# A two-layer hybrid decoder on one core: weighted sums as one 512-column and one 256-column product per head, and four weight granules a layer split by casting and adding DMA

## The chip, the cores and the metric

The kernel runs on one core of one Trainium2 chip. The metric is the time of one execution in device microseconds (us); of several runs the median is given. The profile comes from one execution that the hardware profiler recorded. In it PE is TensorE (matrix products), PEld its loading of weights, DVE is VectorE, ACT is ScalarE, POOL is GpSimd, and SP issues most DMAs.

## The reference, cut to what matters

Two layers, each with a token mixer (two kinds of attention, eight heads each of 64 columns) and a SwiGLU block, both with a residual and a layer norm. There are 256 tokens and 1024 columns, in float32.

```
for l in range(DEPTH):                       # 2
    mix = hybrid_mixer(x, w_in[l], w_branch_sb[l], w_branch_moba[l], w_out[l])
    x = layer_norm(DEEPNORM_ALPHA * x + mix, ...)
    ffn = swiglu(x, w_gate[l], w_up[l], w_down[l])
    x = layer_norm(DEEPNORM_ALPHA * x + ffn, ...)

hybrid_mixer: proj = x @ w_in  ->  q,k,v (stick-breaking) | q,k,v (MoBA) | two gates
    o_sb = weights_sb @ v_sb      # weights_sb: stick-breaking, strictly causal
    o_mb = weights_mb @ v_mb      # weights_mb: softmax, causal (one block of 256)
    merged = sigmoid(g_sb) * (o_sb @ w_branch_sb) + sigmoid(g_mb) * (o_mb @ w_branch_moba)
    return merged @ w_out
```

The change concerns the two weighted sums, `weights @ v`, and the way in which some pieces of the weight matrices get ready.

## The kernel before, in words

**Split operands.** Every float32 operand of a matrix product is split in two parts of the type fp32r: `hi` is the value cast, `lo` is the value minus `hi`. A product is then hi·hi + hi·lo + lo·hi, three matmuls that add into one PSUM bank (`mm3`, line 334).

**Weights.** All weights are laid out by the host as granules of 128 x 1024 floats (512 KB), 122 to a layer, in the order of their use. `WeightStream` (line 100) takes a granule through three steps: SP loads it into one of six `raw` buffers (line 137), ACT casts it into the ring `whi` (line 163), DVE subtracts to give the ring `wlo` (line 167). The rings hold ten granules; a place comes free when the granule that held it has been used (`after`, line 124). Where the weights are the stationary operand (`feat_major`, line 390) a granule takes 24 matmuls of 256 columns; where the tokens are (`tok_major`, line 366) 12 of 512.

**Order.** The program is written out by `Weave` (line 38). The main line issues the projections; attention, rotary embedding, splits and norms are generators that `yield` the time at which they want to go on. The planner advances its own clock with each matmul and keeps planned end times for ACT and DVE, from simple costs (n/1200 + 0.08 us on ACT, n/960 + 0.06 us on DVE). It decides only the order in which instructions are written; on the chip each engine runs its own in that order, and waits on semaphores.

**Attention.** A line treats two pairs of heads (`sb_line` line 505, `mb_line` line 535; two lines of each kind a layer). For each pair: `scores`, then weights on ACT and DVE (in `sb_line` with a small POOL memset of `keep`, line 521, ahead of DVE's scans), then `weighted` (line 460): PE transposes the weights into a bank pair (`_pT`), ACT and DVE split them into `_phi` and `_plo`, and `product_line` (line 479) multiplies. Its stationary operand is v of a head with hi and lo parts side by side, 64 + 64 columns, so that rows 0 to 63 of the result belong to v's hi and rows 64 to 127 to v's lo. A query of the first half sees 128 keys, one of the second half 256. So each head takes four matmuls: the first half of v with 256 columns of `hi`, and with 256 of `lo`; the second half with 128 of each. Both heads of a pair go to one bank `o` of the pool `psC`, which has two banks; the transposes of the rotary embedding, of norms and of SwiGLU take turns in the same two. ACT copies the lower rows (`low`), DVE adds the upper ones (`both`), and the sum is split in its turn.

A tile of 128 x 2 x 384 floats (`wide_work`, tag A, four buffers) holds `keep`, `beta`, `e`, `phi` or `plo` in turn.

Of the kernel before, what the change touches and what calls it, by code (L numbers as in the profile page):

```python
# [7 lines left out]
F32 = mybir.dt.float32  # L8
F32R = mybir.dt.float32r
# [21 lines left out]
NG_LAYER = 122  # L31
EARLY = [*range(8), 8, 14, 9, 15, 20, 24, 21, 25, *range(10, 14), *range(16, 20), 22, 23, *range(26, 40)]
NACT = 12
NWIDE = 4
NTOK_FC = 4


# [62 lines left out]
class WeightStream:  # L100
# [3 lines left out]
    def __init__(self, nc, pool, w, total, weave, rings):  # L104
        self.nc, self.pool, self.w, self.total, self.weave = nc, pool, w, total, weave
        self.loaded, self.split = 0, NWHOLE
        self.done = -1
        self.current = 0
        self.rings = rings
        self._lay()  # L110
        self.dma_t = 1.7
        self.raw, self.parts, self.there, self.ready = {}, {}, {}, {}

    def _lay(self):

# [16 lines left out]
    def load(self, upto, between=lambda g, i: None):  # L132
        while self.loaded < min(upto, self.total):
            g = self.loaded
            t = self.pool.tile([P, GCOLS], F32, tag="raw", name=f"raw{g}", bufs=NRAW)
            for i, sl in enumerate(self._pieces(g)):
                self.nc.sync.dma_start(t[:, sl], self.w[place(g), :, sl])
                between(g, i)
            self.raw[g] = t
            self.dma_t = max(self.dma_t, self.ready.get(g - NRAW, 0.0) + 0.5) + 1.46  # L140
            self.there[g] = self.dma_t + 1.0
            self.loaded += 1

    def line(self):

        nc, weave = self.nc, self.weave
        while self.split < self.total:
            g = self.split
            ahead = g - self.current
            if self.after[g] > self.done:  # L150
                yield weave.t + 0.1
                continue
            if ahead >= LEAD and max(weave.dve_t, weave.act_t) > weave.t + BACKLOG:
                yield weave.t + 0.2
                continue
# [12 lines left out]
            self.parts[g], self.ready[g] = (hi, lo), e
            self.split += 1
            self.load(g + 1 + NRAW)  # L170
# [5 lines left out]
    def take(self, g):  # L176
        self.current = max(self.current, g)
        while self.split <= g:
            self.weave._step(self.side)
        self.weave.t = max(self.weave.t, self.ready[g])  # L180
        return self.parts[g]

# [2 lines left out]
RING = 10 * GCOLS + LINES  # L185
NRAW = 6
NWHOLE = 2
X_AFTER = {(0, 1): ((1, 0), (0, 1)), (1, 1): ((1, 1), (0, 2)), (2, 1): ((1, 2),)}
NSPLIT = 10
HOLD = 8  # L190
# [23 lines left out]
def hybrid_trunk_kernel(ctx: ExitStack, tc: tile.TileContext, w, xT_in, x_in, ln_in,  # L214
# [21 lines left out]
        return work.tile(shape, F32, tag="T", name=name, bufs=3)  # L236

    def wide_work(name, dt=F32):
        return work.tile([P, 2, 384], dt, tag="A", name=name, bufs=NWIDE)

    def bankM(name, shape):
        return psM.tile(shape, F32, tag="M", name=name)

    def bankC(name, shape):
        return psC.tile(shape, F32, tag="C", name=name)

    taken = [False]

    def banksB(name):
        return psB.tile([P, 2, 512], F32, tag="B", name=name)  # L250
# [164 lines left out]
    def rope_line(name, ps, t, put):  # L415

        tmp = small_work(f"{name}_tok{t}", [P, 8, DH])
        e = act(pe_done(), WIDTH, nc.scalar.copy, tmp, ps.rearrange("p (h d) -> p h d", d=DH))
        yield e
        half = ROPE // 2  # L420
        a = small.tile([P, 8, ROPE], F32, tag="ra", name=f"{name}_ra{t}", bufs=1)
        b = small.tile([P, 8, ROPE], F32, tag="rb", name=f"{name}_rb{t}", bufs=1)
        cc = rope[:, t, 0, None, :].to_broadcast([P, 8, ROPE])
        s0 = rope[:, t, 1, None, :half].to_broadcast([P, 8, half])
        s1 = rope[:, t, 1, None, half:].to_broadcast([P, 8, half])
        mul = nc.vector.tensor_mul
        dve(e, P, mul, a, tmp[:, :, :ROPE], cc)
        dve(e, P // 2, mul, b[:, :, :half], tmp[:, :, half:ROPE], s0)
        dve(e, P // 2, mul, b[:, :, half:], tmp[:, :, :half], s1)
        e = dve(e, 2 * P, nc.vector.tensor_add, tmp[:, :, :ROPE], a, b)  # L430
        yield e + MARGIN
        tp = bankC(f"{name}_tp{t}", [P, NPAIR, P])
        flat = tmp.rearrange("p h d -> p (h d)")
        pe_after(e)
        for p in range(NPAIR):
            transpose(tp[:, p, :], flat[:, p * P:(p + 1) * P])
        yield pe_done()
        yield from put(tp, slice(t * P, (t + 1) * P), pe_done())

    PARTS = ((0, P), (P, 384))  # L440

# [18 lines left out]
    def weighted(name, d, wts, v, oT, es, due=None):  # L460

        yield max(es) + MARGIN
        pTs = [banksB(f"{name}_pT{j}") for j in range(2)]
        pe_after(max(es))
        for pT, wt in zip(pTs, wts):
            for h in range(2):
                for c in range(3):
                    cs = slice(c * P, (c + 1) * P)
                    transpose(pT[:, h, cs], wt[:, h, cs])
        e = pe_done()  # L470
        yield e
        for j in range(2):
            parts = [wide_work(f"{name}_p{n}{j}", F32R) for n in ("hi", "lo")]
            e = yield from split_line(*parts, pTs[j][:, :, :384], 768, e)
            if j == 1:
                taken[0] = False
            weave.start(product_line(f"{name}_o{j}", 2 * d + j, parts, v, oT, e, due))

    def product_line(name, p, parts, v, oT, e, due):

        yield e + MARGIN
        while due is not None and len(due) < 2:
            yield weave.t + 0.1
        pe_after(e)
        o = bankC(name, [P, 2, S])
        for h in range(2):
            va, vb = (x[:, 2 * p + h].rearrange("p a c -> p (a c)") for x in v)
            for n, part in enumerate(parts):
                mm(o[:, h, :], va, part[:, h, :S], h == n == 0, False)
            for n, part in enumerate(parts):  # L490
                mm(o[:, h, P:], vb, part[:, h, S:], False, h == n == 1)
        e = pe_done()
        yield e
        if not oT:
            oT.extend(pair_tiles(name[:4] + "o", [P, NPAIR, S]))
        low = small_work(f"{name}_low", [P, 2, S])
        both = small_work(f"{name}_both", [P, S])
        e = act(e, 2 * S, nc.scalar.copy, low[:DH], o[DH:])
        yield e
        for h, r in enumerate(ROWS):  # L500
            e = dve(e, S, nc.vector.tensor_add, both[r], o[:DH, h, :], low[:DH, h, :])
        yield e
        yield from split_line(oT[0][:, p, :], oT[1][:, p, :], both, S, e)

    def sb_line(name, d, q, q_there, ps, v, oT, done):
# [9 lines left out]
        ws_, fs = [], []  # L515
        for s, e in zip(ss, es):
            yield e
            keep, beta = (wide_work(f"{name}_{n}{len(ws_)}") for n in ("keep", "beta"))
            e1 = act(e, 768, nc.scalar.activation, keep, s[:, :, :384], AF.Sigmoid, scale=-1.0)
            e2 = act(e, 768, nc.scalar.activation, beta, s[:, :, :384], AF.Sigmoid)  # L520
            e1 = weave.pool(e1, nc.gpsimd.memset, keep[:, :, P - 1::2 * P], 0.0)
            ws_.append((keep, beta))
            fs.append((e1, e2))
# [11 lines left out]
    def mb_line(name, d, q, k, v, oT, before, done, scored):  # L535
# [16 lines left out]
        for (s, nmax), e in zip(work_, fs):  # L552
            yield e
            ssum = small.tile([P, 2, 2], F32, tag="ssum", name=f"{name}_ssum{len(es)}")
            ex = wide_work(f"{name}_e{len(es)}")
            for h in range(2):
                for n, (a, b) in enumerate(PARTS):
                    e = act(e, b - a + 300, nc.scalar.activation, ex[:, h, a:b], s[:, h, a:b], AF.Exp,
                            bias=nmax[:, h, n:n + 1], accum_out=ssum[:, h, n:n + 1])
            exs.append((ex, ssum))  # L560
            es.append(e)
# [377 lines left out]
```

## Time and profile before

| what | value |
|---|---|
| median of 3 runs (lowest to highest) | 734.23 us (734.13 to 734.25) |
| the profiled execution's own time | 734.21 us |
| its span, first to last instruction | 732.4 us, mean granted PE clock 0.998 |
| busy DVE, ACT, POOL | 515.6, 384.5, 14.8 us |
| DMA issues on POOL | none |
| layer 0: sb lines from the first scores to their last product | about 43 to 81 us |
| layer 0: mb lines | about 90 to 129 us |
| layer 1: the same two | about 402 to 440, 449 to 489 us |

The span is 1.8 us shorter than the time, which also has what lies before the first and after the last instruction. [...] A row of the timeline has its start, its duration, engine, line, operation and operands; `xN` merges N neighbours.

### The profile page before, as it was taken

The page shows a single profiled execution, that of the slowest core. Times are in us where ns is not written, and L with a number is a line of the kernel's source. Part 1 is how long each engine was busy: PE and PEld are TensorE (multiplying, and loading weights), DVE is VectorE, ACT ScalarE, POOL GpSimd, SP SyncE. Part 2 cuts the span into 40 slices and gives each one's busy share as a digit, 9 for nine tenths or more (in the row PEclk, how much of TensorE's full clock was granted, in tenths as well). Part 3 has the DMA queues.
Part 4 walks back from the last instruction along what each step waited for, and adds up shares of the span by engine and source line. Part 5 has one row for each costly group of instructions (what it writes and reads, how often), then busy time and mean ns, then how long its engine had stood idle before and what let it go on. Part 6 is the DMA issues. An engine that isn't in the chain of part 4 may idle for free.

```text
span 732.4 us, 12739 instructions
## 1 busy us (share of the span) xinstructions
PE 723.1 (99%) x5136; PEld 664.7 (91%) x5136; DVE 515.6 (70%) x723; ACT 384.5 (52%) x570; POOL 14.8 (2%) x30
## 2 busy tenths in 40 slices
PE   9999999999999999999999999999999999999996
PEld 5898999998799999988889989999888999998885
DVE  4988877795886666644578897777578766656416
ACT  5755668743565455533356566675246645445300
POOL 0000000000000000000000000000010000000001
PEclk9999999999999999999999999999999999999999
DMA  8953553863586655476158425457436866554601
GB/s 319 353 202 116 163 191 122 263 241 117 176 279 211 198 201 186 160 273 215 57 177 286 144 96 190 147 158 257 161 115 223 264 203 193 186 172 129 244 1 57
DMA packets 39226, 136.32 MB, mean 186 GB/s; under 512 B 4480, under 2 KB 5504, under 8 KB 39168
## 3 DMA queue, kind: packets, MB, share of 16 engines
q1 hardware_dynamic: 39168, 135.51, 54.9%
q8 instruction: 40, 0.66, 0.3%
q14 instruction: 18, 0.15, 0.1%
HBM read 134.45 MB, written 1.05 MB: 185 GB/s over the span
## 4 chain that ended last, share of the span: by engine, by line
PE 95%; DVE 2%; issue 1%; ACT 1%; POOL 1%; POOLq 0%; DVEq 0%
PE l1pf L328 13%; PE l0pf L328 13%; PE l0pd L328 8%; PE l1pg L328 6%; PE l0pg L328 6%; PE l1pe L328 4%; PE l1pd L328 4%; PE l0pq L328 3%; PE l0pk L328 3%; PE l1pk L328 3%; PE l1pvq L328 3%; PE l1pb L328 3%; PE l0pb L328 3%; PE l1pw L328 2%; PE l0pw L328 2%; PE l0pft L328 2%
## 5 line engine op out<-in xcount | busy, mean ns | idle before, releaser
L56 DVE TENSOR_TENSOR wlo<-raw,whi 128x1024 fp32r<-128x1024 f32 (+1 forms) x244 | 292.1, 1214 | 77.1 <-ACT whi L51 74.2
L51 ACT CAST whi<-raw 128x1024 fp32r<-128x1024 f32 (+1 forms) x244 | 249.8, 1042 | 68.4 <-PE l0pd L328 19.1
L328 PE MATMUL l0pf<-xT_hi,whi 128*128 128x256 f32 x288 | 79.6, 276 | 0.0
L328 PE MATMUL l1pf<-xT_hi,whi 128*128 128x256 f32 x288 | 79.6, 276 | 0.0
L328 PE MATMUL l0pf<-xT_lo,whi 128*128 128x256 f32 x288 | 79.5, 276 | 0.0
L328 PE MATMUL l0pf<-xT_hi,wlo 128*128 128x256 f32 x288 | 79.5, 276 | 0.0
L328 PE MATMUL l1pf<-xT_lo,whi 128*128 128x256 f32 x288 | 79.5, 276 | 0.0
L328 PE MATMUL l1pf<-xT_hi,wlo 128*128 128x256 f32 x288 | 79.5, 276 | 0.0
L328 PEld LDWEIGHTS l0pf<-xT_lo,whi 128*128 128x128 f32 x288 | 54.1, 188 | 0.0
L328 PEld LDWEIGHTS l1pf<-xT_lo,whi 128*128 128x128 f32 x288 | 54.1, 188 | 0.0
L328 PEld LDWEIGHTS l1pf<-xT_hi,whi 128*128 128x128 f32 x288 | 54.1, 188 | 0.0
L328 PEld LDWEIGHTS l0pf<-xT_hi,whi 128*128 128x128 f32 x288 | 54.1, 188 | 0.0
L328 PEld LDWEIGHTS l0pf<-xT_hi,wlo 128*128 128x128 f32 x288 | 54.1, 188 | 0.0
L328 PEld LDWEIGHTS l1pf<-xT_hi,wlo 128*128 128x128 f32 x288 | 54.1, 188 | 0.0
L328 PE MATMUL l1pg<-xT_hi,whi 128*128 128x256 f32 x128 | 36.0, 281 | 0.0
L328 PE MATMUL l0pg<-xT_hi,whi 128*128 128x256 f32 x128 | 36.0, 281 | 0.0
L328 PE MATMUL l1pg<-xT_lo,whi 128*128 128x256 f32 x128 | 35.5, 277 | 0.0
L328 PE MATMUL l1pg<-xT_hi,wlo 128*128 128x256 f32 x128 | 35.5, 277 | 0.0
L328 PE MATMUL l0pg<-xT_lo,whi 128*128 128x256 f32 x128 | 35.5, 277 | 0.0
L328 PE MATMUL l0pg<-xT_hi,wlo 128*128 128x256 f32 x128 | 35.4, 277 | 0.0
L328 PE MATMUL l0pd<-whi,l0h_hi 128*128 128x512 f32 x88 | 34.4, 391 | 0.0
L328 PE MATMUL l0pd<-whi,l0h_lo 128*128 128x512 f32 x88 | 34.3, 389 | 0.0
(403 smaller groups left out, 1763.9 us busy)
## 6 DMA issues: line engine op xcount, KB each, us to landing
raw<-in_w_dram SPq DMA_DIRECT2D x240, 512.0 KB, 4.2
ln<-in_ln_dram SPq DMA_DIRECT2D x8, 512.0 KB, 6.2
raw<-in_w_dram SPq DMA_DIRECT2D x8, 256.0 KB, 4.9
x<-in_x_dram SPq DMA_DIRECT2D x2, 512.0 KB, 5.3
out_dram<-x SPq DMA_DIRECT2D x3, 256.0 KB, 2.0
xT_raw<-in_xT_dram SPq DMA_DIRECT2D x4, 128.0 KB, 4.4
xT_raw<-in_xT_dram SPq DMA_DIRECT2D x2, 256.0 KB, 4.8
out_dram<-x SPq DMA_DIRECT2D x2, 128.0 KB, 1.9
```

Of the source, the lines that this page charges most:

```text
L51: f(*args, **kw)
L56: f(*args, **kw)
L328: nc.tensor.matmul(o, a, b, start=start, stop=stop)
```

## The change

It has two parts, and what goes with them.

1. `weighted` makes one tile for hi and lo of a pair, in blocks of 128 columns that alternate (hi, lo, hi, lo, hi, lo). `product_line` then needs two matmuls a head: the first half of v with four blocks (512 columns), the second half with two (256 columns), which add onto the last 256. Each head has a bank to itself, so a product takes both banks of `psC`. The parts come out side by side: DVE adds v_hi·lo to the copied v_lo·hi, and then v_hi·hi; v_lo·lo is dropped. ACT copies 64 x 256 twice in place of 64 x 512 once; DVE makes four additions in place of two.
2. Granules 18, 27, 35 and 43 of each layer are no longer loaded by SP and split by ACT and DVE. POOL issues a casting DMA into `whi`, writes `wlo` = -`whi` with a `tensor_scalar` of 128 x 1024, and issues a DMA that adds the weights onto `wlo`.
3. The planner gets `turnC`, `holdC`, `freeC`: a product is written only once both banks are free in its plan. Tiles of tag A have twice the size and two buffers in place of four; `keep` and `beta` share one.

```
+BY_DMA = (18, 27, 35, 43)
...
+    def by_dma(self, g):
+        return g % NG_LAYER in BY_DMA
+    def dma_line(self, g):
+        nc, weave = self.nc, self.weave
+        hi, lo = self.parts[g]
+        nc.gpsimd.dma_start(hi, self.w[place(g)], max_dma_last_dim=4096)
+        yield weave.t + 4.5
+        e = weave.pool(weave.t, nc.gpsimd.tensor_scalar, lo, hi.bitcast(F32), -1.0, None, op0=OP.mult)
+        yield e + 1.0
+        nc.gpsimd.dma_start(lo, self.w[place(g)], accum_op=OP.add, max_dma_last_dim=4096)
+        self.ready[g] = weave.t + 5.0
...
     def line(self):
         while self.split < self.total:
+            for g in range(max(self.split, NWHOLE), min(self.split + 6, self.total)):
+                if self.by_dma(g) and g not in self.dma and self.after[g] <= self.done:
...
+                    self.dma[g] = weave.add(self.dma_line(g), weave.t)
...
+    def turnC(n=1):
+        while max(held[-2:][:n]) > weave.t:
+            yield weave.t + 0.1
...
-            parts = [wide_work(f"{name}_p{n}{j}", F32R) for n in ("hi", "lo")]
-            e = yield from split_line(*parts, pTs[j][:, :, :384], 768, e)
+            parts = work.tile([P, 2, 6, P], F32R, tag="A", name=f"{name}_p{j}", bufs=NWIDE)
+            e = yield from split_line(parts[:, :, ::2], parts[:, :, 1::2],
+                                      pTs[j][:, :, :384].rearrange("p h (a c) -> p h a c", c=P), 768, e)
...
+        yield from turnC(2)
         pe_after(e)
-        o = bankC(name, [P, 2, S])
-        for h in range(2):
+        os = [bankC(f"{name}{h}", [P, 2, 2, P]) for h in range(2)]
+        own = holdC(2)
+        for h, o in enumerate(os):
+            o = o.rearrange("p a n c -> p (a n c)")
             va, vb = ...
-            for n, part in enumerate(parts):
-                mm(o[:, h, :], va, part[:, h, :S], h == n == 0, False)
-            for n, part in enumerate(parts):
-                mm(o[:, h, P:], vb, part[:, h, S:], False, h == n == 1)
+            mm(o, va, parts[:, h, :4].rearrange("p a c -> p (a c)"), True, False)
+            mm(o[:, S:], vb, parts[:, h, 4:].rearrange("p a c -> p (a c)"), False, True)
...
-        e = act(e, 2 * S, nc.scalar.copy, low[:DH], o[DH:])
+        for h, o in enumerate(os):
+            e = act(e, S, nc.scalar.copy, low[:DH, h], o[DH:, :, 0, :])
         yield e
-        for h, r in enumerate(ROWS):
-            e = dve(e, S, nc.vector.tensor_add, both[r], o[:DH, h, :], low[:DH, h, :])
+        for h, o in enumerate(os):
+            dve(e, S, nc.vector.tensor_add, low[:DH, h], o[:DH, :, 1, :], low[:DH, h])
+        for h, o in enumerate(os):
+            e = dve(e, S, nc.vector.tensor_add, both[ROWS[h]], o[:DH, :, 0, :], low[:DH, h])
+        freeC(own, e)
```

PE at the first product of layer 0 (`l0sb_o`), before; `l0pk` is the projection that runs around it:

```order
L328 MATMUL l0pk_616<-whi,xT_lo 128x512
L328 MATMUL l0sb_o_661<-l0sb_phi_643,l0vsb_166 128x256
L328 MATMUL l0sb_o_661<-l0sb_plo_644,l0vsb_166 128x256
L328 MATMUL l0sb_o_661<-l0sb_phi_643,l0vsb_167 128x128
L328 MATMUL l0sb_o_661<-l0sb_plo_644,l0vsb_167 128x128
L328 MATMUL l0sb_o_661<-l0sb_phi_643,l0vsb_166 128x256
L328 MATMUL l0sb_o_661<-l0sb_plo_644,l0vsb_166 128x256
L328 MATMUL l0sb_o_661<-l0sb_phi_643,l0vsb_167 128x128
L328 MATMUL l0sb_o_661<-l0sb_plo_644,l0vsb_167 128x128
L328 MATMUL l0pk_616<-whi,xT_hi 128x512
```

The same place on PE after the change:

```order
L372 MATMUL l0pk_633<-whi,xT_lo 128x512
L372 MATMUL l0sb_o_662<-l0sb_p_638,l0vsb_166 128x512
L372 MATMUL l0sb_o_662<-l0sb_p_638,l0vsb_167 128x256
L372 MATMUL l0sb_o_663<-l0sb_p_638,l0vsb_166 128x512
L372 MATMUL l0sb_o_663<-l0sb_p_638,l0vsb_167 128x256
L372 MATMUL l0pk_633<-whi,xT_hi 128x512
```

Eight matmuls in one bank have become four in two. The second product of that line followed this one on PE after 3 `l0pk`, 24 score matmuls and 3 `l0pk`; now 6 `l0pk` stand in the last place.

POOL from its first memsets to those of the sb lines of layer 0, before:

```order
L277 MEMSET ends 128x384
L278 MEMSET ends 128x2
L61 MEMSET l0sb_keep_533 128x2x2
L61 MEMSET l0sb_keep_541 128x2x2
L61 MEMSET l0sb_keep_729 128x2x2
L61 MEMSET l0sb_keep_741 128x2x2
L61 ISA
```

And after (the row `ISA` is a setup instruction of POOL that stands ahead of its first arithmetic, which before was that of a norm):

```order
L321 MEMSET ends 128x384
L322 MEMSET ends 128x2
L156 DMA whi<-in_w_dram 128x1024
L61 ISA
L61 TENSOR_SCALAR wlo<-whi 128x1024
L160 DMA wlo<-in_w_dram 128x1024
L61 MEMSET l0sb_kb_529 128x2x2
L61 MEMSET l0sb_kb_536 128x2x2
L61 MEMSET l0sb_kb_738 128x2x2
```

The three steps of granule 18, and the `ISA`, now stand ahead of the memsets of `keep` (now in the tile `l0sb_kb`). In layer 1 granule 18's three steps stand ahead of that layer's memsets in the same way; the steps of granules 27, 35 and 43 follow the memsets.

DVE behind the first product of layer 0, before:

```order
L56 TENSOR_TENSOR l0sb_o_both<-l0sb_o_661,l0sb_o_low 64x256 x2
L56 TENSOR_TENSOR wlo<-raw_425,whi 128x1024
L56 TENSOR_TENSOR l0sb_s_675<-l0sb_s_675,mask 128x4x128
L56 TENSOR_TENSOR l0sb_s_676<-l0sb_s_676,mask 128x4x128
L56 TENSOR_TENSOR l0sbo_lo<-l0sb_o_both,l0sbo_hi 128x256
```

And after:

```order
L56 TENSOR_TENSOR l0sb_o_low<-l0sb_o_662,l0sb_o_low 64x256
L56 TENSOR_TENSOR l0sb_o_low<-l0sb_o_663,l0sb_o_low 64x256
L56 TENSOR_TENSOR l0sb_o_both<-l0sb_o_662,l0sb_o_low 64x256
L56 TENSOR_TENSOR l0sb_o_both<-l0sb_o_663,l0sb_o_low 64x256
L56 TENSOR_TENSOR wlo<-raw_439,whi 128x1024
L56 TENSOR_TENSOR l0sb_s_673<-l0sb_s_673,mask 128x4x128
L56 TENSOR_TENSOR l0sb_s_674<-l0sb_s_674,mask 128x4x128
L56 TENSOR_TENSOR l0sbo_lo<-l0sb_o_both,l0sbo_hi 128x256
```

Two additions have come in ahead of the split of a granule and of the masks of the next scores.

More of the change, by code (lines that the diff above doesn't have):

```diff
@@ L33 @@
 NACT = 12
-NWIDE = 4
+NWIDE = 2
 NTOK_FC = 4
@@ L111, in __init__ @@
         self.dma_t = 1.7
-        self.raw, self.parts, self.there, self.ready = {}, {}, {}, {}
+        self.raw, self.parts, self.there, self.ready, self.dma = {}, {}, {}, {}, {}
     def _lay(self):
@@ L134, in load @@
             g = self.loaded
+            if self.by_dma(g):
+                self.loaded += 1
+                upto += 1
+                continue
             t = self.pool.tile([P, GCOLS], F32, tag="raw", name=f"raw{g}", bufs=NRAW)
@@ L147, in line @@
         while self.split < self.total:
+            for g in range(max(self.split, NWHOLE), min(self.split + 6, self.total)):
+                if self.by_dma(g) and g not in self.dma and self.after[g] <= self.done:
+                    self.parts[g] = tuple(ring[:, self.place[g]:self.place[g] + GCOLS] for ring in self.rings)
+                    self.dma[g] = weave.add(self.dma_line(g), weave.t)
             g = self.split
+            if g in self.dma:
+                self.split += 1
+                continue
             ahead = g - self.current
@@ L179, in take @@
             self.weave._step(self.side)
+        while g in self.dma and g not in self.ready:
+            self.weave._step(self.dma[g])
         self.weave.t = max(self.weave.t, self.ready[g])
@@ L238, in wide_work @@
     def wide_work(name, dt=F32):
-        return work.tile([P, 2, 384], dt, tag="A", name=name, bufs=NWIDE)
+        return work.tile([P, 2, 2, 384], dt, tag="A", name=name, bufs=NWIDE)
     def bankM(name, shape):
@@ L244, in bankC, with holdC, freeC @@
     def bankC(name, shape):
+        held.append(weave.t)
         return psC.tile(shape, F32, tag="C", name=name)
-    taken = [False]
+    taken, held = [False], [0.0, 0.0]
+    def turnC(n=1):
+        while max(held[-2:][:n]) > weave.t:
+            yield weave.t + 0.1
+    def holdC(n=1):
+        held[-n:] = [1e9] * n
+        return range(len(held) - n, len(held))
+    def freeC(own, e):
+        for i in own:
+            held[i] = e
     def banksB(name):
@@ L431, in rope_line @@
         yield e + MARGIN
+        yield from turnC()
         tp = bankC(f"{name}_tp{t}", [P, NPAIR, P])
+        own = holdC()
         flat = tmp.rearrange("p h d -> p (h d)")
@@ L437, in rope_line @@
         yield pe_done()
-        yield from put(tp, slice(t * P, (t + 1) * P), pe_done())
+        e = yield from put(tp, slice(t * P, (t + 1) * P), pe_done())
+        freeC(own, e)
     PARTS = ((0, P), (P, 384))
@@ L495, in product_line @@
             oT.extend(pair_tiles(name[:4] + "o", [P, NPAIR, S]))
-        low = small_work(f"{name}_low", [P, 2, S])
-        both = small_work(f"{name}_both", [P, S])
-        e = act(e, 2 * S, nc.scalar.copy, low[:DH], o[DH:])
+        low = small_work(f"{name}_low", [P, 2, 2, P])
+        both = small_work(f"{name}_both", [P, 2, P])
+        for h, o in enumerate(os):
+            e = act(e, S, nc.scalar.copy, low[:DH, h], o[DH:, :, 0, :])
         yield e
-        for h, r in enumerate(ROWS):
-            e = dve(e, S, nc.vector.tensor_add, both[r], o[:DH, h, :], low[:DH, h, :])
+        for h, o in enumerate(os):
+            dve(e, S, nc.vector.tensor_add, low[:DH, h], o[:DH, :, 1, :], low[:DH, h])
+        for h, o in enumerate(os):
+            e = dve(e, S, nc.vector.tensor_add, both[ROWS[h]], o[:DH, :, 0, :], low[:DH, h])
+        freeC(own, e)
         yield e
+        both = both.rearrange("p a c -> p (a c)")
         yield from split_line(oT[0][:, p, :], oT[1][:, p, :], both, S, e)
@@ L517, in sb_line @@
             yield e
-            keep, beta = (wide_work(f"{name}_{n}{len(ws_)}") for n in ("keep", "beta"))
+            two = wide_work(f"{name}_kb{len(ws_)}")
+            keep, beta = two[:, 0], two[:, 1]
             e1 = act(e, 768, nc.scalar.activation, keep, s[:, :, :384], AF.Sigmoid, scale=-1.0)
@@ L554, in mb_line @@
             ssum = small.tile([P, 2, 2], F32, tag="ssum", name=f"{name}_ssum{len(es)}")
-            ex = wide_work(f"{name}_e{len(es)}")
+            ex = wide_work(f"{name}_e{len(es)}")[:, 0]
             for h in range(2):
```

## The prediction

> **What bounds the kernel now.** I read the page first: busy times, granted clock, the chain.
>
> ```profile
> PE 723.1 (99%) x5136; PEld 664.7 (91%) x5136; DVE 515.6 (70%) x723; ACT 384.5 (52%) x570; POOL 14.8 (2%) x30
> PEclk9999999999999999999999999999999999999999
> PE 95%; DVE 2%; issue 1%; ACT 1%; POOL 1%; POOLq 0%; DVEq 0%
> ```
>
> PE is busy for 99% of the span at full clock, and 95% of the chain that ended last is PE. A busy PE is not yet a PE at its peak, so the next view is that of PE's waits; these two rows are all of it behind the start.
>
> ```profile
> PE l0a_tp L341 <- DVE xT_lo L56: 0.3, 1, 0.3
> PE l1a_tp L341 <- DVE xT_lo L56: 0.3, 1, 0.3
> ```
>
> PE waits 0.6 us for others in 732.4 us. So a microsecond of PE work that goes is a microsecond of time, as long as nothing else becomes late; and no gain is to be had from DVE or ACT alone.
>
> **The products on PE.** The timeline of PE at the first product of layer 0:
>
> ```profile
> 57.41 0.39 PE L328 MATMUL l0pk<-wlo,xT_hi 128*128 128x512 f32 x1
> 57.64 0.39 PE L328 MATMUL l0pk<-whi,xT_lo 128*128 128x512 f32 x1
> 57.87 0.28 PE L328 MATMUL l0sb_o<-l0sb_phi,l0vsb 128*128 128x256 f32 x1
> ...
> 58.74 0.45 PE L328 MATMUL l0pk<-whi,xT_hi 128*128 128x512 f32 x1
> 59.02 0.40 PE L328 MATMUL l0pk<-wlo,xT_hi 128*128 128x512 f32 x1
> 59.26 0.39 PE L328 MATMUL l0pk<-whi,xT_lo 128*128 128x512 f32 x1
> ```
>
> and at the last product of layer 1:
>
> ```profile
> 487.35 0.28 PE L328 MATMUL l1pg<-xT_lo,whi 128*128 128x256 f32 x1
> 487.46 0.28 PE L328 MATMUL l1pg<-xT_hi,wlo 128*128 128x256 f32 x1
> 487.57 0.28 PE L328 MATMUL l1mb_o<-l1mb_phi,l1vmb 128*128 128x256 f32 x1
> ...
> 488.45 0.34 PE L328 MATMUL l1pg<-xT_hi,whi 128*128 128x256 f32 x1
> 488.62 0.28 PE L328 MATMUL l1pg<-xT_lo,whi 128*128 128x256 f32 x1
> ```
>
> From start to start a 512-column matmul takes 0.23 us and a 256-column one 0.113 us. A product takes 58.74 - 57.87 = 0.87 and 488.45 - 487.57 = 0.88 us, for 1536 columns in all, which at the pitch of the long matmuls would be 0.68. The matmul behind it is late as well: 0.28 us to its successor in place of 0.23, and 0.17 in place of 0.113, so some 0.06 more. The excess fits a weight load per matmul that a 128-column matmul is too short to cover. The new product is 2 x 0.227 + 2 x 0.113 = 0.68 us for the same columns, with every load behind at least 256 columns. There are 16 (two lines of two kinds, two pairs each, two layers; in this tile 32 matmuls make four of them):
>
> ```profile
> L328 PE MATMUL l0sb_o<-l0sb_phi,l0vsb x16: 220/252/332, 57.9 to 80.4; 128*128 128x256 f32 x8, 128*128 128x128 f32 x8
> L328 PE MATMUL l0sb_o<-l0sb_plo,l0vsb x16: 272/280/283, 58.0 to 80.5; 128*128 128x256 f32 x8, 128*128 128x128 f32 x8
> L56 DVE TENSOR_TENSOR l0sb_o_both<-l0sb_o,l0sb_o_low x8: 413/417/418, 59.6 to 81.9; 64x256 f32<-64x256 f32 x8
> L51 ACT COPY l0sb_o_low<-l0sb_o x4: 583/584/584, 58.9 to 80.8; 64x512 f32<-64x512 f32 x4
> ```
>
> Saved: at most 16 x (0.87 + 0.06 - 0.68) = **4.0 us**; if the tail of 0.06 stays and a 512-column matmul costs 0.24, as from 59.02 to 59.26, 16 x (0.87 - 0.70) = 2.7 us. I take 4.0, since pitches of 0.227 and 0.113 hold wherever these shapes follow each other.
>
> **DVE and ACT.** DVE gets two more additions a product, 32 x 0.417 = 13.3 us; ACT two copies for one. A copy of 64 x 256 is not in the trace; the nearest are 0.584 above and this activation of 256 columns:
>
> ```profile
> L51 ACT ACTIVATE l0sf<-l0pf 128x256 f32<-128x256 f32 x18 | 6.9, 385 | 32.2 <-PE l0pf L328 32.2
> L56 DVE TENSOR_TENSOR wlo<-raw,whi 128x1024 fp32r<-128x1024 f32 x240 | 289.4, 1223 | 76.7 <-ACT whi L51 73.8
> L51 ACT CAST whi<-raw 128x1024 fp32r<-128x1024 f32 x240 | 247.4, 1049 | 68.1 <-PE l0pd L328 19.1 <-PE l1pe L328 16.9 <-PE l0pf L328 13.2
> ```
>
> So ACT gets 16 x (2 x 0.385 - 0.584) = 3 us. The eight granules that go to DMA take 8 x 1.223 = 9.8 us off DVE and 8 x 1.049 = 8.4 off ACT. Net DVE +3.5, ACT -5.4: both far under the PE time, so I cost them at nothing, except where PE waits for one product's banks. The tightest place is the second product of a line. After the first ends (57.87 + 0.68 = 58.55), its banks come free after a hop of 0.2, two copies (0.77), four additions (1.67) and two hops: about 61.4. On PE six `l0pk` now stand between scores and second product where three stood:
>
> ```profile
> 61.95 0.27 PE L328 MATMUL l0sb_o<-l0sb_phi,l0vsb 128*128 128x256 f32 x1
> ```
>
> That start moves to 61.95 - 0.25 + 3 x 0.227 = 62.4, so 1 us is left. For the first line this covers the added 0.83 us of additions; without that cover it costs what is missing, once a second product. The smaller number of tag A buffers costs nothing: a line's split parts are written only behind its transposes, which have freed both tiles.
>
> **POOL.** New there: 16 DMA issues, eight `tensor_scalar` of 128 x 1024, and the setup instruction moved forward. Rows that come near:
>
> ```profile
> 0.72 0.42 POOL L277 MEMSET ends<- 128x384 f32 x1 [0.29 <-POOLq L925]
> 1.19 0.10 POOL L278 MEMSET ends<- 128x2 f32 x1
> 46.10 0.11 POOL L61 MEMSET l0sb_keep<- 128x4 f32 x1 [44.80 <-ACT l0sb_keep L51]
> 173.50 1.41 DVE L56 SCALAR_TENSOR_TENSOR x<-x,l0a_nmu,ln 128x512 f32<-128x512 f32 x2 [1.31 <-ACT l0pw L51]
> 173.56 0.75 POOL L61 TENSOR_SCALAR l0a_ve<-l0a_ve 128x1 f32<-128x1 f32 x1 [108.07 <-ACT l0pw L51]
> 405.00 0.11 POOL L61 MEMSET l1sb_keep<- 128x4 f32 x1 [34.37 <-ACT l1sb_keep L51]
> 57.04 0.42 SPq L322 DMA_DIRECT2D x<-in_x_dram  x1
> raw<-in_w_dram SPq DMA_DIRECT2D x240, 512.0 KB, 4.2
> ln<-in_ln_dram SPq DMA_DIRECT2D x8, 512.0 KB, 6.2
> ```
>
> A `tensor_scalar`: 0.32 us for 382 more columns is 0.84 ns a column, so 0.75 + 0.86 = 1.6 us; bounds 0.75 (128 x 1) and 2.5 (columns at twice the price, being read and written). An issue: 0.42 on SP; I take 1 us on POOL, bounds 0.4 and 2. Landing of 512 KB: 4.2 to 6.2 from SP; with a cast I take 5, bounds 4.2 and twice 6.2. The setup is bounded by nothing (the row lies behind 108 us of idle POOL); I take it as hidden behind the landing that follows it.
>
> The place where this can matter is granule 18, whose steps stand ahead of the `keep` memsets. Its ring place comes free when granule 9 has been used, at the first row of each pair here; the second is the last `beta`, the third where PE's transposes of it stand (in layer 0 now at 53.11, since three matmuls ahead of them went behind):
>
> ```profile
> 35.01 0.28 PE L328 MATMUL l0pk<-xT_hi,whi 128*128 128x256 f32 x1
> 50.93 0.96 DVE L56 TENSOR_TENSOR l0sb_beta<-l0sb_beta,l0sb_keep 128x767 f32<-128x767 f32 x1
> 53.11 0.40 PE L328 MATMUL l0pk<-whi,xT_hi 128*128 128x512 f32 x1
> 394.48 0.28 PE L328 MATMUL l1pk<-xT_hi,whi 128*128 128x256 f32 x1
> 409.83 0.96 DVE L56 TENSOR_TENSOR l1sb_beta<-l1sb_beta,l1sb_keep 128x767 f32<-128x767 f32 x1
> 412.58 1.47 PE L341 MATMUL l1sb_pT<-ident,l1sb_beta 128*128 128x128 f32 x12
> ```
>
> The steps on POOL: 35.2 + 1 + 5 + 1.6 + 1 = 43.8, ahead of the memset at 46.10; the memset itself may be 53.11 - 51.89 - 0.2 = 1.0 us late before PE waits. That is a budget of 11.9 us for an estimate of 8.6. Layer 1: from 394.7 to 405.00, plus 412.58 - 410.79 - 0.2 = 1.6, again 11.9. The second DMA lands near 49; PE first uses granule 18 behind 12 transposes (1.3 us) and 12 matmuls, near 57. The other three start some 25 us ahead of use, behind the memsets. Cost: nothing, or one for one beyond the budget.
>
> [...]
>
> **The sum.** 734.2 (the profiled execution; span 732.4 and 1.8 around it; the median is 734.23) - 4.0 + 0.3 for short bank waits = **730.5 us**.
>
> **Rivals.**
>
> *The banks eat the gain.* The planner believes in 0.33 us for an addition (256/960 + 0.06) and 0.29 for a copy where rows show 0.417 and 0.385. For four and two of them it is 0.54 us short; its matmul of 256 columns is 0.109 where 0.113 is measured, which gives back some 0.16 us over the 4 us between two products. Eight second products x 0.38 = 3.0 us; without the allowance of 0.3 that gives 730.2 + 3.0 = 733.2. Against it: the same planner has the same errors now, and PE waits 0.6 us.
>
> *POOL's queue (slower).* If the casting DMA lands in 12.4 us, the steps take 16 us, 4.1 beyond the budget: `keep` is cleared late, DVE's scans stand still with every split queued behind them, and PE waits at the transposes in both layers: 730.5 + 8.2 = 738.7. It decides from steps of 13.8 us on, where 2 x 1.9 eats the gain. For it: no DMA of POOL is in the trace. Against it: two landings of 512 KB are, at 4.2 and 6.2.
>
> *POOL and DVE in each other's way (slower).* The `tensor_scalar` of one column took 0.75 us and ended at 174.31, just as the first of the two DVE operations beside it (173.50 to about 174.25) did. If they exclude each other, DVE loses up to 1.6 us at each of eight, 13 us; uncovered, 743. Cover: DVE idles 76.7 us ahead of splits. [...]
>
> *The matmuls don't get cheaper.* A product stays at 0.93 us, and only additions come in: 734.5. Against it stand all rows of 512 columns.
>
> **How the numbers follow.** Forecast, 729.6 to 732.0: 0.68. Banks, 732.0 to 734.2: 0.12, half of it faster and half same. POOL's queue, 733 to 741: 0.10, of it 0.03 same. Exclusion, or a granule that lands late: 0.05, of it 0.01 same. Matmuls as dear: 0.05, of it 0.03 same. A measurement of this kernel can tell 0.2%, 1.5 us. Faster 0.68 + 0.06 = 0.74; same 0.06 + 0.03 + 0.01 + 0.03 = 0.13; slower 0.13. The range takes in the first two cases, 0.80: 729.6 (the largest saving, no wait, and 0.6 for tails that I may have misjudged) to 734.2.
>
> **What would show it.** Right: 64 matmuls fewer, a product of 0.68 us from start to start, no more than 1 us of PE waits, DVE busy about 519 us, ACT about 379, POOL's memset still near 46 and 405. Wrong: PE waiting at `_o` for DVE (banks), at `sb_pT` for DVE with POOL behind it (queue), at `l0pk` or `l0pg` for a DMA (late granule), or `wlo` rows of DVE well above 1.22 us (exclusion). A `tensor_scalar` over 4.9 us, or a landing over 8.3, would use up the budget by itself.

## The result and the profile after

The changed kernel takes 730.43 us (median of 6 runs, 730.03 to 730.97), the kernel before beside it 734.29 us (6 runs, 734.13 to 735.05): a ratio of 0.9945, 95% interval 0.9933 to 0.9958. The profiled execution took 730.52 us with a span of 728.7. The forecast was 730.5.

The page of the changed kernel: busy times, the granted clock over the span, the chain that ended last.

```profile
PE 719.2 (99%) x5072; PEld 659.3 (90%) x5072; DVE 519.1 (71%) x747; ACT 378.8 (52%) x578; POOL 51.2 (7%) x54
PEclk9999999999999999999999999999999999999999
PE 95%; DVE 2%; issue 1%; ACT 1%; POOL 1%; POOLq 0%; DVEq 0%
```

PE has 64 matmuls and 3.9 us less; DVE and ACT stand at 519 and 379 us. The view of PE's waits (us in total, times, longest) has no wait at a product's banks, none at a transpose behind POOL, and none for a DMA:

```profile
PE l0a_tp L385 <- DVE xT_lo L56: 0.3, 1, 0.3
PE l1a_tp L385 <- DVE xT_lo L56: 0.3, 1, 0.3
PE l0qmb_tp L385 <- issue: 0.2, 1, 0.2
```

The timeline of PE at the first product of layer 0, in the branch projections, and at a product of the last line of layer 1 (start, duration, engine, line, operation, operands; x4 is four neighbours in one row). A row of 0.40 us (512 columns) or 0.28 (256) overlaps the next, which starts 0.24 or 0.12 later, so what a matmul costs is read from start to start:

```profile
57.99 0.39 PE L372 MATMUL l0pk<-whi,xT_lo 128*128 128x512 f32 x1
58.22 0.85 PE L372 MATMUL l0sb_o<-l0sb_p,l0vsb 128*128 128x512 f32 x4
58.91 0.40 PE L372 MATMUL l0pk<-whi,xT_hi 128*128 128x512 f32 x1
59.15 0.40 PE L372 MATMUL l0pk<-wlo,xT_hi 128*128 128x512 f32 x1
...
154.73 0.28 PE L372 MATMUL l0pb<-l0mbo_hi,wlo 128*128 128x256 f32 x1
...
155.52 0.28 PE L372 MATMUL l0pb<-l0sbo_hi,whi 128*128 128x256 f32 x1
...
484.01 0.88 PE L372 MATMUL l1mb_o<-l1mb_p,l1vmb 128*128 128x512 f32 x4
484.73 0.28 PE L372 MATMUL l1pg<-xT_hi,whi 128*128 128x256 f32 x1
484.85 0.28 PE L372 MATMUL l1pg<-xT_lo,whi 128*128 128x256 f32 x1
```

A product now takes 58.91 - 58.22 = 0.69 and 484.73 - 484.01 = 0.72 us, where it took 0.87 and 0.88. The matmul behind it is no longer 0.06 us late: 0.24 and 0.12 to its successor. Summed from start to start over all matmuls of a tile, the sixteen products fell from 14.13 to 11.46 us, the gate projections `pg` of both layers from 89.20 to 88.12; other tiles changed by 0.2 at most. Together that is the shorter span. Of the 1.08 us in `pg` some 0.4 lies right behind the products. The other 0.6 is a matter of pitch: before, 134 of its matmuls, in three stretches (84.0 to 89.9, 443.5 to 449.4 and 463.2 to 467.3), started 117.8 ns apart; after the change those places run at 113.3, the other pitch of this shape (see the experiments).

The groups of additions and copies of one kind of line (count, then busy us and mean ns, then idle before it):

```profile
L56 DVE TENSOR_TENSOR l0sb_o_both<-l0sb_o,l0sb_o_low 64x256 f32<-64x256 f32 x8 | 3.3, 413 | 0.1
L56 DVE TENSOR_TENSOR l0sb_o_low<-l0sb_o,l0sb_o_low 64x256 f32<-64x256 f32 x8 | 3.0, 413 | 1.1 <-ACT l0sb_o_low L51 1.1
L51 ACT COPY l0sb_o_low<-l0sb_o 64x256 f32<-64x256 f32 x8 | 2.8, 371 | 3.6 <-PE l0sb_o L372 3.6
L56 DVE TENSOR_TENSOR wlo<-raw,whi 128x1024 fp32r<-128x1024 f32 x232 | 280.4, 1223 | 77.5 <-ACT whi L51 74.8
```

POOL's timeline at granule 18 of both layers (in brackets the idle time before an instruction and what ended it):

```profile
33.36 0.77 POOL L156 DMA_DIRECT2D whi<-in_w_dram  x1 [32.06 <-PE l0pq L372]
40.83 3.59 POOL L61 TENSOR_SCALAR wlo<-whi 128x1024 fp32r<-128x1024 f32 x1 [6.70 <-DMA whi<-in_w_dram]
44.74 0.93 POOL L160 DMA_DIRECT2D wlo<-in_w_dram  x1 [0.32 <-POOL wlo L61]
45.90 0.10 POOL L61 MEMSET l0sb_kb<- 128x4 f32 x1 [0.23 <-ACT l0sb_kb L51]
...
390.01 0.61 POOL L156 DMA_DIRECT2D whi<-in_w_dram  x1 [21.01 <-PE l1pq L372]
397.26 3.35 POOL L61 TENSOR_SCALAR wlo<-whi 128x1024 fp32r<-128x1024 f32 x1 [6.63 <-DMA whi<-in_w_dram]
```

In layer 0 the three steps take 45.67 - 33.36 = 12.3 us, not the 8.6 estimated, and more than the budget of 11.9. The `tensor_scalar` takes 3.6 us instead of 1.6, the landing of the cast 7 instead of 5. Still the memset waits for ACT, not for POOL: the steps began at 33.4 instead of 35.2, since the place of granule 18 in the ring overlaps granule 9 by 48 columns only and is given back while PE is still at granule 9.

### The profile page after: what moved, and what is told of

Same layout as the page of the kernel before. It is cut to its first block, busy times and chain, and to the rows that moved or that the text cites. A ratio compares the mean times of both kernels' runs of the same rounds, so it can differ in the third digit from the quotient of the medians.

```text
span 728.7 us, 12686 instructions
## 1 busy us (share of the span) xinstructions
PE 719.2 (99%) x5072; PEld 659.3 (90%) x5072; DVE 519.1 (71%) x747; ACT 378.8 (52%) x578; POOL 51.2 (7%) x54
## 4 chain that ended last, share of the span: by engine, by line
PE 95%; DVE 2%; issue 1%; ACT 1%; POOL 1%; POOLq 0%; DVEq 0%
PE l1pf L372 13%; PE l0pf L372 13%; PE l0pd L372 8%; PE l1pg L372 6%; PE l0pg L372 6%; PE l1pe L372 4%; PE l1pd L372 4%; PE l0pq L372 3%; PE l1pk L372 3%; PE l0pk L372 3%; PE l1pvq L372 3%; PE l0pb L372 3%; PE l1pb L372 3%; PE l1pw L372 2%; PE l0pw L372 2%; PE l1pft L372 2%
## 5 line engine op out<-in xcount | busy, mean ns | idle before, releaser
L56 DVE TENSOR_TENSOR wlo<-raw,whi 128x1024 fp32r<-128x1024 f32 (+1 forms) x236 | 283.0, 1214 | 78.4 <-ACT whi L51 75.7
L51 ACT CAST whi<-raw 128x1024 fp32r<-128x1024 f32 (+1 forms) x236 | 242.2, 1042 | 69.5 <-PE l0pd L372 19.7
```

The costliest lines, as they stand in the source:

```text
L51: f(*args, **kw)
L56: f(*args, **kw)
```

## The experiments

All ran beside the kernel before on their chip (734.30 to 734.73 us there). "The changed kernel" is the one of the result.

### One part without the other

**Products alone.** Edit of the changed kernel:

```
-BY_DMA = (18, 27, 35, 43)
+BY_DMA = ()
```

> The new products and banks alone; every granule is again loaded by SP and split by ACT and DVE. Theory (the gain is PE time of the products, and the granules only pay for DVE's additions, which PE does not wait for): 730.1 to 731.0 us, PE waits under 1 us, DVE about 529 us. Rival (without the granules DVE's 13 us of additions in the mixer make PE wait for splits or banks): 732 to 734 us, with PE waits of 1.5 us or more in the mixer stages.

Measured: 739.31 us (5 runs, 738.39 to 740.22), ratio 1.0066 (1.0054 to 1.0079): slower than the kernel before, and outside both expectations. PE's waits:

```profile
PE l0pg L372 <- ACT whi L51: 2.6, 1, 2.6
...
PE l1pb L372 <- ACT whi L51: 1.0, 1, 1.0
PE l1pb L372 <- DVE wlo L56: 1.0, 1, 1.0
PE l0pg L372 <- DVE wlo L56: 0.5, 1, 0.5
```

PE waits for granules, in each layer at one place. ACT's timeline ahead of the first wait:

```profile
113.10 0.22 ACT L51 ACTIVATION_READ_ACCUMULATOR l0mb_e<-l0mb_s,l0mb_nmax 128x1 f32 x1
116.98 0.37 ACT L51 ACTIVATE l0mb_e<-l0mb_s,l0mb_nmax 128x128 f32<-128x128 f32 x1 [3.66 <-issue]
...
119.68 1.28 ACT L51 ACT_TABLE_LOAD   x1
120.97 0.60 ACT L51 ACTIVATE l0gate<-l0pg 128x512 f32<-128x512 f32 x1
121.46 1.04 ACT L51 CAST whi<-raw 128x1024 fp32r<-128x1024 f32 x1
```

The last row is the cast of granule 35, which PE needs at 119.8. It stands in ACT's queue behind the eight exps of the second MoBA line, and in their middle ACT stands still for 3.66 us with nothing named: the exps write a tag-A tile, and of the two the free one is held by split parts that the product at 116 still reads. Behind the stall PE runs at half clock for a while (windows: from and to, length, busy time and count of PE, PEld, DVE, ACT and POOL, then granted clock, the DMA engines' busy share and GB/s):

```profile
119.50:127.00 7.50, 4.44 (x22) 3.95 (x21) 4.32 (x9) 4.74 (x7) 0.00 (x0) 0.68 0.20 70
127.00:135.00 8.00, 8.00 (x61) 7.91 (x61) 5.53 (x9) 4.46 (x9) 0.00 (x0) 0.87 0.31 94
```

The clock stands at 0.5 from 122.2 to 129.0. So 5.1 us of waits and 6.8/2 = 3.4 of clock take back more than the products give. In layer 1 the late granule is 41: its cast at 502.76 stands behind four sigmoids of the gate, which take 2.18 us from 500.68.

**Granules by DMA alone.** The kernel before with `by_dma`, `dma_line` and their callers from the change.

> The products of before, with one bank a pair of heads, and granules 18, 27, 35 and 43 of each layer split by DMA. Theory: nothing of PE changes, so 734.0 to 734.6 us, DVE about 506 us, ACT about 376 us. Rival 1 (the relief of DVE and ACT is worth time): 731 to 733 us. Rival 2 (POOL's queue or the DMAs cost time that the products' gain hides in the whole change): 735 us or more.

Measured: 735.08 us (11 runs, 734.28 to 735.35), ratio 1.0006 (0.9997 to 1.0015). The median lies at the edge of the second rival, but beside the 734.53 of the kernel before, in an interval that contains no change, it shows no price of POOL's queue or the DMAs, and PE's waits are those of before. Relief of DVE (509 us busy) and ACT (377) alone brings nothing. The two parts are thus not additive: +4.8 and +0.5 us (the latter within the noise) by themselves, -3.9 together.

### The price of the products

**The 512-column product as two of 256.**

```
-            mm(o, va, parts[:, h, :4].rearrange("p a c -> p (a c)"), True, False)
+            mm(o[:, :S], va, parts[:, h, :2].rearrange("p a c -> p (a c)"), True, False)
+            mm(o[:, S:], va, parts[:, h, 2:4].rearrange("p a c -> p (a c)"), False, False)
```

> The whole change, but the 512-column matmul of each head is made as two of 256: six matmuls a product in place of four, for the same 1536 columns and with the same order on every engine. Theory (the saving is that no matmul is shorter than the load of the next one's weights): 730.3 to 730.8 us, a product of 0.69 to 0.71 us. Rival (each matmul has a fixed price, 64 fewer of them made 3.9 us): 32 more matmuls cost 1.9 us, 732.4 us, a product of 0.81 us.

Measured: 733.82 us (11 runs), ratio 0.9993 (0.9983 to 1.0002), above both expectations. The products still behave as the theory says, 0.70 to 0.72 us each (0.82 behind scores) and 11.63 in all. What was lost lies elsewhere, in PE's timeline of the branch projections, at the place shown above:

```profile
154.75 0.28 PE L372 MATMUL l0pb<-l0sbo_hi,whi 128*128 128x256 f32 x1
...
155.58 0.28 PE L372 MATMUL l0pb<-l0mbo_lo,whi 128*128 128x256 f32 x1
```

Seven starts on, 0.83 us have gone, where the changed kernel takes 155.52 - 154.73 = 0.79. Streams of 256-column matmuls run at one of two pitches, 113.3 or 117.8 ns. In all fourteen traces an unbroken stream keeps its pitch, up to 845 matmuls long; it changes only where a product, scores, transposes, another shape or a wait come between. Here `pg` takes 44.99 us a layer instead of 44.06 and `pb` 22.61 instead of 21.76: 3.6 us in both layers, which is the loss. What sets the pitch stays open.

**The 256-column product as two of 128.**

```
-            mm(o[:, S:], vb, parts[:, h, 4:].rearrange("p a c -> p (a c)"), False, True)
+            mm(o[:, S:S + P], vb, parts[:, h, 4], False, False)
+            nc.tensor.matmul(o[:, S + P:], vb, parts[:, h, 5], start=False, stop=True)
```

> The whole change, but the 256-column matmul of each head is made as two of 128: six matmuls a product, the same columns and the same order. Theory (a 128-column matmul is too short to cover the next load of weights): each head loses about 0.06 us at the second 128-column matmul and 0.055 at the next one, 32 x 0.115 = 3.7 us, 734.2 us, a product near 0.87 us. Rival (a fixed price for each matmul): 1.9 us, 732.4 us, the same as with two of 256.

Measured: 733.62 us (11 runs), ratio 0.9990 (0.9982 to 0.9999), between the two. The products take 13.90 us in all (0.85 to 0.86 each, 0.96 behind scores), almost what they took before, and the matmul behind is late again (0.288 and 0.170 us). So it is the 128-column matmuls that made a product dear, as the prediction had it; 64 of them in place of 32 of 256 columns cost 2.4 us in the products and 0.8 behind them in `pg`, which is the whole loss.

### POOL's queue

One more `tensor_scalar` on granule 18 of each layer, behind its own and ahead of the adding DMA, and in the second kernel two (`range(2)`):

```
+        if g % NG_LAYER == 18:
+            for _ in range(1):
+                nc.gpsimd.tensor_scalar(lo, hi.bitcast(F32), -1.0, None, op0=OP.mult)
```

> The whole change, with one more tensor_scalar of granule 18 on POOL (the same values written again, twice in all), in each layer; all other orders are unchanged. In the changed kernel the memset of keep starts at 45.90 and 403.37 us with POOL free since 45.67 and 401.82; the last beta ends 1.6 us before PE's transposes of it in both layers, once 0.2 us for the signal is taken off. Theory (POOL's queue stalls DVE's scans and then PE, one for one beyond that slack): with 2.8 to 3.2 us more, PE waits 1.0 to 1.6 us at sb_pT in layer 0 and under 0.3 in layer 1, time 731.4 to 732.2 us. Rival (DVE and PE have other slack there): 730.4 us, no wait at sb_pT.

> As before, with two more tensor_scalar of granule 18 in each layer (three in all). Theory: 5.6 to 6.4 us more on POOL make PE wait 3.8 to 4.8 us in layer 0 and 2.3 to 3.3 us in layer 1, time 736.5 to 738.5 us. Rival (other slack): under 733 us.

Measured: 731.30 us (5 runs, 730.51 to 731.75) with one and 738.88 us (5 runs, 737.96 to 739.51) with two, 0.1 us below and 0.4 above what the theory gave. The waits fit less well. With one, the first memset comes at 48.7 instead of 45.9 and PE waits 0.2 us at `l0sb_pT` where the theory had 1.0 to 1.6; the cover is used up there. With two, POOL's timeline, then PE's waits, then the windows over the stall of layer 0 and behind the stalls of both layers:

```profile
43.68 6.47 POOL L161 TENSOR_SCALAR wlo<-whi 128x1024 fp32r<-128x1024 f32 x2
50.47 0.93 POOL L163 DMA_DIRECT2D wlo<-in_w_dram  x1 [0.32 <-POOL wlo L161]
51.09 0.47 POOL L61 MEMSET l0sb_kb<- 128x4 f32 x2
```

```profile
PE l0sb_pT L388 <- DVE l0sb_kb L56: 2.6, 2, 1.9
PE l1sb_pT L388 <- DVE l1sb_kb L56: 1.9, 1, 1.9
```

```profile
54.00:57.00 3.00, 0.85 (x6) 0.64 (x6) 2.90 (x4) 2.08 (x3) 0.00 (x0) 1.00 0.41 82
58.20:61.60 3.40, 3.40 (x9) 2.62 (x9) 3.40 (x5) 1.74 (x2) 0.00 (x0) 0.50 0.49 146
420.00:423.40 3.40, 3.40 (x10) 2.63 (x9) 3.40 (x5) 1.50 (x2) 0.00 (x0) 0.50 0.55 160
```

This is the rival of POOL's queue as the prediction drew it: memset late, DVE's scans late, PE waiting at the transposes in both layers. Its price is made up otherwise: 2.6 and 1.9 us of waits instead of 3.8 to 4.8 and 2.3 to 3.3, and behind each stall 3.4 us at half clock, 1.7 us lost each time, which the theory had not. That the time came out near it is in part luck.

### Why the products need the DMA granules

Three theories: the two tag-A buffers hold ACT up; the two granules that are late (35 and 43) are what counts; DVE's queue has no room for the added additions.

**The two tiles `e` of a MoBA line share one tag-A tile**, so that the next line's exps wait for the first product only. No engine's order changes; without DMA granules and with them.

```
-            ex = wide_work(f"{name}_e{len(es)}")[:, 0]
+            if not es:
+                two = wide_work(f"{name}_e")
+            ex = two[:, len(es)]
```

> The wide products without the DMA granules, as in the run that took 739.3, but the two tiles e of a MoBA line share one tag-A tile, so that the next line's exps wait only for the split parts of the first product and no longer for those of the late second one. Every engine's instructions stand in the same order as in that run. Theory (the buffers make ACT's late cast): ACT's idle stretch of 3.7 us ahead of the exps near 117 falls below 1 us, PE's wait at l0pg for whi (2.6 us) and the stretch at half clock behind it go, time 730.5 to 733 (the wait of about 2 us at l1pb behind the sigmoids of the gate may stay). Rival (the relief of ACT and DVE by the DMA granules is what counts, wherever it falls): the stall stays, 737.5 to 739.5.

> The changed kernel with the two tiles e of a MoBA line in one tag-A tile, nothing else; same order on every engine. Theory: ACT's idle stretch near 117 goes here too, but the granules that come by DMA cover it already and PE waits for nothing, so 730.4 +- 0.5. Rival (the stretch still costs something that the waits of PE do not show): below 729.8.

Measured without DMA granules: 735.84 us (10 runs, 734.09 to 737.09), between both expectations; ACT's idle stretch is gone, PE still waits:

```profile
PE l1pb L372 <- ACT whi L51: 1.0, 1, 1.0
PE l1pb L372 <- DVE wlo L56: 1.0, 1, 1.0
PE l0pg L372 <- DVE wlo L56: 0.8, 1, 0.8
```

So the buffers cost 739.31 - 735.84 = 3.5 us of what the products alone lose; in the two traces the waits go from 5.1 to 3.0 us, and the rest is clock. The spread follows the clock: the three runs below 735 us have a mean clock of 0.997, the seven above it 0.994 to 0.995. With DMA granules: 730.13 us (4 runs, 729.79 to 730.32), ratio 0.9942 (0.9927 to 0.9957) beside 0.9945 for the changed kernel, the same within both intervals; the stretch is gone there too and had cost nothing.

**Only two of the four granules by DMA**, 35 and 43, or 18 and 27.

> The changed kernel with granules 35 and 43 alone by casting and adding DMA; 18 and 27 go through SP, ACT and DVE as before the change. Theory (what counts is which granule is late): the late casts near 120 and 503 are those behind 35 and 43, so PE waits no more than 1 us and the time is 730.0 to 731.5, with DVE near 522 and ACT near 382. Rival (the sum of the relief counts): half of the way between 739.3 and 730.4, 734 to 736.

> The changed kernel with granules 18 and 27 alone by casting and adding DMA; 35 and 43 go through SP, ACT and DVE. Theory: the casts near 120 and 503 are late as without any DMA granule, PE waits about 3 us at l0pg and 2 at l1pb, with a stretch at half clock behind the first: 737 to 739.5. Rival (the sum of the relief counts): 734 to 736.

Measured: 731.27 us (4 runs, 730.97 to 732.15) with 35 and 43, as the theory had it, and PE waits for no granule; 733.71 us (10 runs, 732.58 to 734.10) with 18 and 27, which misses both expectations. There the wait at `l0pg` is gone although granule 35 goes through ACT and ACT's stretch (3.65 us, near 116.8) is there. PE waits later:

```profile
PE l1pw L372 <- DVE wlo L56: 0.8, 1, 0.8
PE l0pw L372 <- DVE wlo L56: 0.8, 1, 0.8
```

`pw`, the output projection, takes 1.2 and 1.5 us longer than in the changed kernel. So not single granules count, nor the sum of the relief alone. The written order of ACT fits this. What stands around the block of eight exps (here left out) in the products alone:

```
L51 CAST whi_89<-raw33_934 128x1024
L51 CAST whi_89<-raw34_965 128x1024
...
L51 ACT_TABLE_LOAD
L51 ACTIVATE l0gate2_1279<-l0pg4_1280 128x512
L51 CAST whi_89<-raw35_1022 128x1024
```

and with granules 18 and 27 by DMA:

```
L51 CAST whi_89<-raw36_953 128x1024
L51 CAST whi_89<-raw37_982 128x1024
...
L51 ACT_TABLE_LOAD
L51 ACTIVATE l0gate2_1289<-l0pg4_1290 128x512
L51 CAST l0mbo_hi_1269<-l0mb0_o1_both_1363 128x256
L51 CAST whi_89<-raw38_1036 128x1024
```

Before the change 36 and 37 stand ahead of the block as well, in the changed kernel 37 and 38. With the products alone the planner writes the splits three granules later, and 35 falls behind the block. It was not its load that was late: with the products alone granule 35 had landed at 98.29, 23 us ahead of its cast, and ACT was busy for 4.83 of the 10 us from 105 to 115. On the chip the order becomes the lead: the start of the first matmul that uses a granule, minus the end of its `wlo` (for granule 35 with the products alone 122.55 - 123.76, from the rows of PE and DVE). In us, layer 0:

| granule | before | changed | products alone | 18 and 27 by DMA |
|---|---|---|---|---|
| 24 | 11.0 | 25.4 | 8.6 | 25.5 |
| 30 | 14.0 | 16.4 | 2.6 | 16.4 |
| 35 | 14.7 | DMA | -1.2 | 14.2 |
| 40 | 12.2 | 8.6 | 2.4 | 3.2 |
| 48 | 16.5 | 5.7 | 3.0 | 0.2 |

The lead is a stock. The products draw it down from some 14 us; each granule by DMA puts some back, and what 18 and 27 put back is used up again by the forties. Behind granule 48 `pw` goes on to the next granule every 6 matmuls instead of 12. There the lead falls to -1.1 us at granule 49 with 18 and 27 by DMA, which is the wait at `pw`, and in the changed kernel to 1.5 at granule 52 of both layers (11.1 before, in layer 0): its stock is nearly used up too.

**Two additions a product instead of four**, with the planner still counting four, so that no order changes; with shared `e` and without, no DMA granules.

```
-            dve(e, S, nc.vector.tensor_add, low[:DH, h], o[:DH, :, 1, :], low[:DH, h])
+            dve(e, S, lambda *x: None, low[:DH, h], o[:DH, :, 1, :], low[:DH, h])
```

> No DMA granules, the two tiles e of a MoBA line in one, and two additions a product on DVE as before the change: the addition of v_hi by w_lo is left out of the result, all else stands in the same order on every engine. Theory (through the mixer DVE's queue has no room: each 0.41 us of added additions puts the splits of granules off by as much, and the stock of split granules ahead of PE is eaten up): 16 additions a layer, 6.6 us, come back as lead, the lead over PE at granules 36 to 50 of layer 0 rises from 0 to 3 us to 5 us or more, PE waits under 0.5 us at l0pg and l1pb, time 729.8 to 731.5. Rival (the granules are late for another reason, their casts behind ACT's other work): no change against the same kernel with four additions, 735 to 737.

> No DMA granules, tag-A buffers as in the changed kernel, and two additions a product (v_hi by w_lo left out of the result, all else in the same order). Theory (the stock of split granules decides, and the 3.7 us for which ACT waits for a tag-A tile are covered as soon as the stock is there): 730.0 to 732.5, with that idle stretch of ACT near 117 still in the trace. Rival (the buffers put the cast off whatever the stock): PE waits 2 to 3 us at l0pg for whi, 734.5 to 737.

Measured: 736.18 us (10 runs, 734.48 to 737.62), as its rival had it, and 739.90 us (4 runs, 739.43 to 740.01), above both expectations. DVE is busy for 10 us less than with the products alone (526.0 there), and PE waits as it did there. The busy times and the longest wait of the second kernel:

```profile
PE 723.6 (98%) x5072; PEld 662.8 (90%) x5072; DVE 515.4 (70%) x723; ACT 386.4 (52%) x586; POOL 14.8 (2%) x30
```

```profile
PE l0pg L372 <- ACT whi L51: 2.6, 1, 2.6
```

The lead at granules 30 and 35 stays at 2.6 and -1.2. The theory that DVE lacks room falls: with the order unchanged, DVE's work can go and not a microsecond comes back. What is left is where their casts are written, and the tag-A buffers in addition; this is read from the orders and the early landing of granule 35, for no kernel moved a cast alone. That the planner writes them later because it counts the new additions and copies as backlog fits its rule (a granule two or more ahead waits while DVE's or ACT's plan stands more than 0.37 us ahead of PE's), but no kernel changed those costs alone, so this last step was not tried.

## Why the prediction was right, point by point

- **A microsecond of PE is a microsecond of time, as long as nothing else becomes late.** Right here: the span fell by 3.65 us, and PE's matmuls from start to start account for it.
- **The product at 0.68 us, 4.0 us saved.** Nearly: 0.690 behind 512-column rows, 0.713 behind 256-column ones, 0.808 for the two behind scores (0.977 before). That saved 2.7 us in the products and 0.8 in the matmuls right behind them, 3.5 where 4.0 stood. Another 0.6 came from the stretches of `pg` that ran at 117.8 ns before and not after; the prediction had no term for them, and its pitch of 0.113 does not hold wherever this shape follows itself. Some 0.4 went in other projections, most of it in `pq` and `pv`. That these and the bank waits below add up to the forecast within 0.1 us is luck. The cause that the prediction only found to fit, matmuls of 128 columns, is borne out by splitting one back (13.90 us for the products where the changed kernel has 11.46). In the trace before, the weight loads of the first product start 0.11 to 0.12 us apart from 57.87 to 58.56, where 128 columns at the pitch of the long matmuls would take 0.057.
- **0.3 us for bank waits.** None came. An addition took 0.413 us and a copy 0.371, as estimated. The cover was larger than the one microsecond estimated: the last addition of the first product ends at 60.71, and the second product starts at 62.78. (The prediction's own steps add up to 61.6, not 61.4, with hops of 0.2, as from 58.74 to the copy at 58.94 before.)
- **DVE +3.5, ACT -5.4.** Measured 519.1 - 515.6 = +3.5 and 378.8 - 384.5 = -5.7.
- **POOL's steps, 8.6 us against a budget of 11.9.** The mechanism was right and two terms were too small: a `tensor_scalar` of 128 x 1024 took 2.8 to 3.6 us (bounds 0.75 to 2.5, so outside them) and this landing about 7. By that budget 12.3 us would have been late by 0.4, had the ring place not come free 1.8 us sooner. The budget was too small as well: with one more `tensor_scalar` the memset came 2.8 us later and PE waited 0.2, so about 2.6 us of cover stood where the prediction counted 1.0. One more costs 0.9 us in all, two 8.5.
- **The setup hidden behind the landing.** The trace shows no extra: POOL waits 6.70 us for the first landing in layer 0, where the setup instruction stands, and 6.63 in layer 1, where none does.
- **POOL and DVE in each other's way.** Seen, but not where it would hurt: in the changed kernel no `wlo` row of DVE rose above 1.229 us, and the rows that were lengthened lost 0.8 us, not 1.6. More on this below.
- **No gain is to be had from DVE or ACT alone.** Right by itself (+0.5 us). But the prediction costed the granules at nothing in the sum too, and that step failed: the 730.5 holds only with them, and that they do what the products need is luck as far as the prediction goes. The forecast reached the right time with a part of the change treated as a mere relief that in truth pays for the other part: products alone take 739.3. The prediction read PE's 0.6 us of waits as slack and did not measure the stock behind it, nor where the order puts the casts once the planner's load changes.
- **The smaller number of tag A buffers costs nothing.** Wrong as a mechanism. The split parts do find free tiles, but the next line's `e` waits for them; 3.5 us with the products alone. It costs nothing in the changed kernel, because the lead covers ACT's 3.65 us.

## What to carry to other kernels

When PE never waits, ask how much lead stands behind that: for a stream of prepared operands, take the end of each preparation against its first use, stage by stage, and see what the edit draws from it. In a program whose order a planner writes, added work on an engine with room may put off other steps by its planned cost (not tried here by itself); comparing the orders around long blocks shows where steps have moved, busy times do not. A short stall of PE may cost nearly twice its length, here 1.9 us as a wait and 1.7 as clock.

## What the hardware showed beyond expectation

- **Half clock behind short stalls.** With two more `tensor_scalar` the granted clock was 0.50 from 58.2 to 61.6 and from 420.0 to 423.4, so for 3.4 us once in each layer; with the products alone for 6.8 us, from 122.2 to 129.0, twice as long. PE had not been idle all the while ahead of it: of the 3.4 us up to the fall it had been busy for 1.2 with the products alone (until 119.96), and for 1.5 with two more in layer 0, where it had gone on at 57.35 after a wait of 1.93 us. What decides on the fall and its length stays open.
- **Two pitches of 256-column matmuls**, 113.3 and 117.8 ns, each kept until something else comes between.
- **Casting and adding DMAs of POOL.** The DMA issues of the changed kernel (median us to landing at the end):

```profile
raw<-in_w_dram SPq DMA_DIRECT2D x232, 512.0 KB, 4.3
whi<-in_w_dram POOLq DMA_DIRECT2D x8, 512.0 KB, 4.3
wlo<-in_w_dram POOLq DMA_DIRECT2D x8, 512.0 KB, 6.3
```

A cast lands as fast as a plain load at the median (3.6 to 7.3), an addition 2 us later (5.5 to 7.6).

- **POOL beside DVE.** In the trace of the changed kernel they hold each other up in part: POOL's `tensor_scalar` takes 2.77 us when a `wlo` subtraction of DVE starts in its course (1.226 us, not slowed), and up to 3.59 when one is under way at its start; one DVE row in each layer, which starts 0.2 us behind POOL's, takes 1.26 us instead of 0.42. In three of the other kernels single `wlo` rows were lengthened as well: from 1.23 to 2.06 us with the 512-column product as two of 256 (at 39.05) and with two more `tensor_scalar` (40.86), and to 2.06 and 2.08 with the 256-column product as two of 128 (40.36 and 453.35). Each lost 0.83 to 0.85 us, less than the 2.8 to 3.8 that POOL's instruction took.
